# Eight PSUM banks in one ring during the visits of the second feed-forward product

## The chip, the cores and the metric

The kernel runs on one core of one Trainium2 chip. The metric is the device time of one execution in microseconds (us). Three runs of the kernel before gave 1599.46, 1599.53 and 1602.58 us; the median is 1599.53 us. One further execution was profiled, and all views of the trace come from it.

## The reference

The reference is one layer of an encoder, applied to two sequences of 512 tokens with 1024 features each. A normalized input goes through three branches (a state-space scan, a differential attention, a cross attention to a memory), these are gated and merged, and a feed-forward block follows. The change lies in the product with `w_ffn_out`, in the last line of this cut:

```
def _layer(x, mem, l, p):
    ...
    x = x + merged @ p['w_out'][l]
    xn2 = _rmsnorm(x, p['norm_ffn'][l])
    gate, up = jnp.split(xn2 @ p['w_ffn_in'][l], 2, axis=-1)
    return x + (jax.nn.silu(gate) * up) @ p['w_ffn_out'][l]
```

`w_ffn_in` is 1024 x 5632, `w_ffn_out` is 2816 x 1024, all in fp32. The result of the layer is normalized once more and is the output.

## The kernel before

Every fp32 product is made of three matmuls (high x high, high x low, low x high), for which ScalarE casts an operand to its high part (L134, L137) and VectorE subtracts to get the low part (L135, L138). TensorE is called PE below, VectorE DVE, ScalarE ACT, GpSimd POOL, and SP is the engine that issues all DMAs, in one queue.

The two sequences stand side by side as 1024 columns, so that both feed-forward products are 2 x 2 block products. They are done with seven block products in place of eight (a Strassen-Winograd scheme): the list `SEVEN` names them A11, S2, A12, S3, S1, A22, S4. Each of the seven needs a PSUM bank of 128 x 512 fp32 of its own; below they are called products 0 to 6.

- First product (22 steps `i`): seven products of four contraction tiles each. The last step (`i == KFF - 1`) runs its tiles outermost, like a visit, and takes six banks from the ring `mm` and the seventh from the ring `tr` (by `aux()`).
- Second product: twelve *visits* (`VISITS`). A visit is one block of output features with two to four *pairs* of contraction tiles; in each pair all seven products get three matmuls, so a pair is 21 matmuls. Its seven banks are six of `bank()` (ring `mm`) and one of `aux()` (ring `tr`).
- End: the last four contraction tiles, which are no pairs, are done by ordinary tiles of one bank each, over all eight blocks of output features, first for 512 columns, then twice for 256. They take their banks from `bank()`, and each is added to the output `y` by DVE at L1346.

At the end of each visit the seven banks are emptied by `quadrants` (L1104 on): ACT copies product 0 (L1108, `p`), and DVE makes six sums and one second read at L1102, in this order: product 1 (`u`), product 2 (`gf`), product 3 (`u`), product 4 (`p`), product 4 again (`up`), product 5 (`nsq`), product 6 (`nsq`). POOL adds the four results to `y` (L1275).

PSUM has eight banks of this size. Before the change they stand as a ring of six named `mm` and a ring of two named `tr` from the merging stage to the end of the kernel. Because a visit takes six of `mm` and one of `tr`, each `mm` bank comes up again for the product of the same number in the next visit, and a `tr` bank in every second visit. A matmul that opens a bank waits until the last read of what the bank held is done (`reuse_waits="tile"`).

Weights of a pair come from DRAM, in two loads: `wa` (L1225, 384 KB, for A11, A12, A22) and `ws_` (L1223, 512 KB, for the four S). The first 16 pairs are prepared whole, the next 12 in part, the last 8 are split on the spot. A pair's operands `th`, `tl` come from tiles `aD` that the first product wrote to DRAM (L1169) and that are read back at L1121 and L1122.

The order of instructions on each engine is made by a scheduling pass over the program's dependences. For PE, `PE.on = True` holds the order in which the kernel text issues matmuls, from the last step of the first product to the last visit. The other engines' order, and SP's queue, are the pass's own.

Of the kernel before, what the change touches and what calls it, by code (L numbers as in the profile page):

```python
# [72 lines left out]
def encoder(ctx: ExitStack, tc: tile.TileContext, a, out):  # L73
# [19 lines left out]
    def open_banks(**tags):  # L93

        bank_es.close()
        for tag, n in tags.items():
            pools[tag] = bank_es.enter_context(tc.tile_pool(name=tag, bufs=n, space=PSUM, reuse_waits="tile"))

    bank_es = ExitStack()

    open_tags(ctx, ld=4)
    xp_es, phase = ExitStack(), ExitStack()
# [3 lines left out]
    def slot(tag, shape=(P, NT), dt=F32, name="sl"):  # L106
        return pools[tag].tile(list(shape), dt, tag=tag, name=name)

    def bank(tag="mm"):
        return pools[tag].tile([P, 512], F32, tag=tag, name="bk" + tag)  # L110

    def aux():
        return bank("tr")


    ident = cst.tile([P, P], F32, name="ident")
# [14 lines left out]
    def split(hi, lo, src, scale=None):  # L131

        if scale is None:
            h = S.copy(hi, src)  # L134
            l_ = V.tensor_tensor(out=lo, in0=src, in1=hi.bitcast(F32), op=ALU.subtract)  # L135
        else:
            h = S.activation(out=hi, in_=src, func=AF.Copy, scale=scale)  # L137
            l_ = V.scalar_tensor_tensor(out=lo, in0=src, scalar=scale, in1=hi.bitcast(F32), op0=ALU.mult, op1=ALU.subtract)  # L138
        return h, l_
# [47 lines left out]
    def rstd(acc, n, nt=4):  # L187


        ss = aux()  # L190
        for t in range(nt):
            PE.matmul(ss[:, t : t + 1], acc[:, t * P : (t + 1) * P], onec[:, 0:1], start=(t == 0), stop=(t == nt - 1))
        return factor(ss, n, nt)

    def factor(ss, n, nt=4, bias=epsc):

        rs = rp.tile([P, 4], F32, tag="rs", name="rs", bufs=4)
        S.activation(out=rs[:, :nt], in_=ss[:, :nt], func=AF.Sqrt, scale=1.0 / n, bias=bias)
        V.reciprocal(rs[:, :nt], rs[:, :nt])
        bc = aux()  # L200
        for t in range(nt):
            PE.transpose(bc[:, t * P : (t + 1) * P], rs[:, t : t + 1].broadcast_to([P, P]), ident)
        return rs, bc

    open_banks(mm=4, tr=4)
    bD = drp.tile([3, 4, P, NT], F32, name="bD")
    gD = drp.tile([24, P, NT], F32, name="gD")
    mD = drp.tile([4, P, 2, L], F32, name="mD")  # L210
    yD = drp.tile([512, T, NS, NC], F32, name="yD")
    uD = drp.tile([512, T, NS, NC], F32, name="uD")
    kx = Ctx()
    kx.__dict__.update(tc=tc, nc=nc, a=a, slot=slot, open_tags=open_tags, aux=aux, drp=drp, ident=ident, vcol=vcol, uD=uD, yD=yD)
    s5 = s5_gen(kx)
    next(s5)
# [76 lines left out]
    def queued():  # L293

        return tc.issue_after(last_w.ins)
# [286 lines left out]
    memory(1)  # L582

    open_banks(mm=2, sc=3, tr=2, oo=1)
    open_tags(phase, xT=4)
    xa = phase.enter_context(tc.tile_pool(name="xa", bufs=2, reuse_waits="tile"))
# [104 lines left out]
    for i in range(-AHEAD, len(steps) + 1):  # L691
# [14 lines left out]
        if 0 <= i < len(steps):  # L706
# [4 lines left out]
            tr = aux()  # L711
# [215 lines left out]


    open_banks(mm=6, tr=2)
    open_tags(phase, ms=16)  # L930
    ves = ExitStack()
# [46 lines left out]
    def quad_room(i):  # L978
        j = i // 2 % 2
        return slot(f"th{j}", [P, 7, L], F32R, "th"), slot(f"tl{j}", [P, 7, L], F32R, "tl")  # L980
# [3 lines left out]
    def quad_split(i, xa_, xb_, t_):  # L984

        nonlocal last_q
        th, tl = quad_room(i)
        split(th[:, 0], tl[:, 0], xa_[:, 0:L])
        split(th[:, 1:3].rearrange("p a n -> p (a n)"), tl[:, 1:3].rearrange("p a n -> p (a n)"), xb_)
        split(th[:, 3:5], tl[:, 3:5], t_[:, 0:2])  # L990
        last_q = split(th[:, 5:7], tl[:, 5:7], t_[:, 2:4])
        return th, tl
# [112 lines left out]
    def quadrants(ps, p0, other=("up", "gf")):  # L1105

        p1 = ap2.tile([P, L], F32, tag="p1", name="p1")
        S.copy(p1, p0)  # L1108
        u2 = summed("u2", next(ps), p1)
        c11 = summed("gf", next(ps), p1, 2)  # L1110
        u3 = summed("u3", next(ps), u2)
        p5 = next(ps)
        u4 = summed("p1", p5, u2)
        c22 = summed("up", p5, u3, 2)
        c21 = summed(other[0], next(ps), u3, 2)
        return c11, summed(other[1], next(ps), u4, 2), c21, c22

    def act_pair(p, tag="ts", third=PO):

        xa_, xb_ = slot("ld", name="fa"), slot("ld", name="fb")  # L1120
        nc.sync.dma_start(xa_, aD[2 * p])  # L1121
        nc.sync.dma_start(xb_, aD[2 * p + 1])  # L1122
        return xa_, xb_, quad_sums(xa_, xb_, tag, third)
# [60 lines left out]
    def pair_in():  # L1184
        pairs.append(quad_split(len(pairs), *act_pair(len(pairs))))
# [8 lines left out]
    def keep(n):  # L1194
        if not kept:
            lasts.extend(quad_room(NPAIR + 1))
        for _ in range(n):
            i = len(kept)
            if i % 2 == 0:
                lasts[2:] = [slot("ld", [P, 2, L], name="fw")]  # L1200
            k0, k1, raw = lasts
            with queued():
                nc.sync.dma_start(raw[:, i % 2], last_rows(i + 1))
            kept.append((k0[:, i], k1[:, i], raw[:, i % 2]))
# [39 lines left out]
    with queued():  # L1244
        nxt = act_pair(2, third=V)
    n_p = 0
    for v, (m, lo_, hi_) in enumerate(VISITS):
        ps = [bank() for _ in range(6)] + [aux()]
        for p in range(lo_, hi_):
            if n_p + 2 < len(pieces):  # L1250
                next(coming[n_p + 2])
            for g in coming[n_p + 1 : n_p + 2]:
                for _ in g:
                    pass
            th, tl = pairs[p]
            w = made[n_p]
            n_p += 1
            if v < 4 and p == 1:
                with queued():
                    for t in (m, m + 4):  # L1260
                        nc.sync.dma_start(y[t], x1D[t])
            for p_, (nm, o) in zip(ps, SEVEN):
                wh, wl = w[nm]
                PE.matmul(p_, wh, th[:, o], start=(p == lo_), stop=False)
                PE.matmul(p_, wh, tl[:, o], start=False, stop=False)
                PE.matmul(p_, wl, th[:, o], start=False, stop=(p == hi_ - 1))
            if v == 3 and p == 0:
                pair_in()
            if (v, p) in ((10, 7), (10, 8), (11, 7), (11, 8)):
                keep(1 if v == 10 and p == 7 else 2)  # L1270
        ps = iter(ps)
        c11, c12, c21, c22 = quadrants(ps, next(ps), ("nsq", "nsq"))
        for c_, t, s in ((c11, 0, 0), (c22, 4, 1), (c21, 4, 0), (c12, 0, 1)):
            yv = y[m + t][:, s * L : (s + 1) * L]
            PO.tensor_tensor(out=yv, in0=yv, in1=c_, op=ALU.add)  # L1275
        if v == 0:
            with tc.issue_after(last_sum.ins):
                pairs.append(quad_split(2, *nxt))
        elif v == 1:
            with queued(), tc.issue_after(last_sum.ins):  # L1280
                pair_in()
        for _ in range({3: 1, 4: 1, 6: 1, 7: 1}.get(v, 0)):
            pair_in()
        if v == 8:

            r0, r1 = quad_room(NPAIR)
            r2 = slot("ts", [P, 4, L], F32R, name="r2")
            room = [(r0[:, 2 * i : 2 * i + 2], r1[:, 2 * i : 2 * i + 2]) for i in range(3)] + [(r2[:, 0:2], r2[:, 2:4])]
            ah, al = [], []
            for i in range(2 * NPAIR, KFF):  # L1290
                ac = slot("ld", name="fl")
                nc.sync.dma_start(ac, aD[i])
                th, tl = (r_.rearrange("p a n -> p (a n)") for r_ in room[i - 2 * NPAIR])
                split(th, tl, ac, scale=0.5)
                ah.append(th)
                al.append(tl)
    PE.on = False


    def ones(ss, sq, n, start=False, stop=False):  # L1300
# [492 lines left out]
```

## Time and profile before

| | us |
|---|---|
| median of three runs | 1599.53 |
| the profiled execution, its own time | 1599.28 |
| span of its profile | 1597.5 |
| PE busy in it | 1579.1 |
| DVE busy in it | 1163.7 |
| ACT, POOL busy in it | 636.8, 542.6 |
| first matmul of the visits, in us from the span's start | 1360.88 |
| first matmul of the end stage | 1538.82 |

Times in a timeline row are the start in us from the span's start and the length in us; then the engine, the line of the kernel, the operation, what is written from what is read, the shape and the count. In brackets stands how long the engine was idle before, and whose end released it. `bkmm` and `bktr` are banks of the two rings. The length of a matmul is its time through a pipeline: the next starts about 0.23 us after it, so an idle time in brackets is shorter than the step that was lost. `x2` means two neighbours merged into one row.

### The profile page before, as it was taken

Reading aid. Unit: us, or ns where it says so; the run is one execution under the profiler, and the core shown is the slowest. Engines: PE = TensorE matmul, PEld = TensorE weight load, DVE = VectorE, ACT = ScalarE, POOL = GpSimd, SP = SyncE. Lnnn points to the kernel's source line nnn. Section 1 sums busy time; section 2 is a strip of 40 time slices with the busy share of each in tenths; the row PEclk is TensorE's granted clock in tenths of the full one; section 3 lists DMA queues with packets and bytes.
Section 4 is the critical chain, followed back from the end, with each engine's and each line's share of the span. In section 5 each row is a group of like instructions: output and inputs, shape, how many; then the busy total and the mean of one; then the engine's idle time right before and its main releaser. Section 6 shows DMA issues by size and latency. Waiting matters only on the chain.

```text
span 1597.5 us, 21606 instructions
## 1 busy us (share of the span) xinstructions
PE 1579.1 (99%) x7838; PEld 1314.8 (82%) x7838; DVE 1163.7 (73%) x1856; ACT 636.8 (40%) x1140; POOL 542.6 (34%) x449
## 2 busy tenths in 40 slices
PE   9999999999999999999999999999999999999997
PEld 7888788888898789878878878888888888788877
DVE  7976997067774776775365578888898778998654
ACT  6544313265552465573123443323333224233323
POOL 0010100001333220300443366666665553444553
PEclk9999999999999999999999999999999999999999
DMA  9544523676762111253454432333332223985222
GB/s 366 174 159 152 175 94 123 182 261 213 262 224 102 46 55 40 73 178 133 138 190 140 144 108 89 123 122 129 119 116 109 81 91 115 355 332 196 75 67 106
DMA packets 104890, 237.84 MB, mean 149 GB/s; under 512 B 13520, under 2 KB 45008, under 8 KB 104784
## 3 DMA queue, kind: packets, MB, share of 16 engines
q1 hardware_dynamic: 104784, 236.47, 43.4%
q8 instruction: 61, 1.00, 0.2%
q14 instruction: 45, 0.37, 0.1%
HBM read 165.16 MB, written 71.27 MB: 148 GB/s over the span
## 4 chain that ended last, share of the span: by engine, by line
PE 89%; DVE 5%; issue 2%; DMA 2%; POOL 1%; ACT 1%; SPq 0%; POOLq 0%; DVEq 0%; ACTq 0%
PE bkmm L66 78%; PE bktr L66 3%; DVE tl L135 2%; PE bkoo L66 2%; PE bktr L69 2%; PE bksc L66 1%; PE bktr L1627 1%; PE bktr L1598 1%; PE bktr L1688 0%; PE bktr L1686 0%; PE bktr L1687 0%; PE bktr L1566 0%; DMA acc<-in_w_fo 0%; DMA mt<-in_memT 0%; DMA fl<-aD 0%
## 5 line engine op out<-in xcount | busy, mean ns | idle before, releaser
L66 PE MATMUL bkmm<-xh,wh 128*128 128x512 f32 x640 | 254.7, 398 | 0.0
L66 PE MATMUL bkmm<-xh,wl 128*128 128x512 f32 x640 | 251.1, 393 | 0.0
L66 PE MATMUL bkmm<-xl,wh 128*128 128x512 f32 x640 | 250.5, 391 | 0.0
L66 PE MATMUL bkmm<-tl,wh 128*128 128x512 f32 (+1 forms) x621 | 241.3, 389 | 1.4 <-DVE tl L135 1.4
L66 PE MATMUL bkmm<-th,wl 128*128 128x512 f32 (+1 forms) x621 | 241.1, 389 | 1.0 <-DVE wl L135 1.0
L66 PE MATMUL bkmm<-th,wh 128*128 128x512 f32 (+1 forms) x621 | 241.3, 389 | 0.0
L134 ACT CAST wh<-wf 128x1024 fp32r<-128x1024 f32 (+1 forms) x134 | 117.9, 880 | 220.8 <-PE bkmm L66 183.2
L135 DVE TENSOR_TENSOR wl<-wf,wh 128x1024 fp32r<-128x1024 f32 (+1 forms) x134 | 146.5, 1093 | 48.8 <-ACT wh L134 33.5
L66 PE MATMUL bkmm<-th,w 128*128 128x512 f32 x432 | 141.4, 392 | 3.5 <-DVE up L1102 2.0
L66 PEld LDWEIGHTS bkmm<-xh,wl 128*128 128x128 f32 x640 | 120.2, 188 | 26.6 <-issue 1.3
L66 PEld LDWEIGHTS bkmm<-xh,wh 128*128 128x128 f32 x640 | 120.4, 188 | 26.4 <-issue 3.4
L66 PEld LDWEIGHTS bkmm<-xl,wh 128*128 128x128 f32 x640 | 120.5, 188 | 22.6 <-issue 0.4
L66 PEld LDWEIGHTS bkmm<-tl,wh 128*128 128x128 f32 x621 | 116.6, 188 | 26.2 <-DVE tl L135 2.1
L66 PEld LDWEIGHTS bkmm<-th,wl 128*128 128x128 f32 x621 | 116.6, 188 | 25.6 <-DVE wl L135 1.9
L66 PEld LDWEIGHTS bkmm<-th,wh 128*128 128x128 f32 x621 | 116.6, 188 | 23.7
L1166 POOL TENSOR_TENSOR up<-up,acc 128x512 f32<-128x512 f32 x44 | 84.2, 1931 | 87.4 <-DVE up L1102 87.4
L454 POOL TENSOR_TENSOR raw<-raw 128x128 f32<-128x128 f32 x28 | 15.2, 546 | 285.0 <-DVE nb L545 206.5
L66 PEld LDWEIGHTS bkmm<-th,w 128*128 128x128 f32 x432 | 80.9, 188 | 24.9 <-DVE up L1102 4.5
L793 POOL TENSOR_TENSOR mg<-mg,gl 128x1024 f32<-128x1024 f32 x16 | 43.5, 2720 | 138.1 <-DVE gl L789 138.1
L66 PE MATMUL bkmm<-tl,w 128*128 128x512 f32 x216 | 84.2, 390 | 0.0
L66 PE MATMUL bkmm<-yh,wh 128*128 128x512 f32 x192 | 75.9, 397 | 0.8 <-DVE gl L789 0.8
L1165 ACT ACTIVATE ac<-gf 128x512 f32<-128x512 f32 x44 | 27.8, 633 | 122.5 <-DVE gf L1164 63.5
(651 smaller groups left out, 3580.8 us busy)
## 6 DMA issues: line engine op xcount, KB each, us to landing
wf<-in_w_in SPq DMA_DIRECT2D x40, 512.0 KB, 4.1
wD<-hl SPq DMA_DIRECT2D x28, 512.0 KB, 2.9
w<-wD SPq DMA_DIRECT2D x28, 512.0 KB, 4.8
gD<-gt SPq DMA_DIRECT2D x24, 512.0 KB, 2.8
gl<-gD SPq DMA_DIRECT2D x24, 512.0 KB, 3.4
wf<-in_w_fg SPq DMA_DIRECT2D x22, 512.0 KB, 3.7
wf<-in_w_fu SPq DMA_DIRECT2D x22, 512.0 KB, 3.6
aD<-ac SPq DMA_DIRECT2D x22, 512.0 KB, 3.0
```

Of the source, the lines that this page charges most:

```text
L66: return self.put(self.eng.matmul(*args, **kw))
L69: return self.put(self.eng.transpose(*args, **kw))
L134: h = S.copy(hi, src)
L135: l_ = V.tensor_tensor(out=lo, in0=src, in1=hi.bitcast(F32), op=ALU.subtract)
L454: PO.tensor_tensor(out=a22, in0=a21, in1=a22, op=ALU.add)
L793: PO.tensor_tensor(out=mg[m], in0=mg[m], in1=gt, op=ALU.add)
L1165: last_t = S.activation(out=ac[:, cs], in_=gf, func=AF.Tanh, scale=0.5)
L1166: PO.tensor_tensor(out=up, in0=up, in1=accs[s], op=ALU.mult)
L1598: PE.matmul(kp[64 * hf : 64 * hf + 48, g * 144 : (g + 1) * 144], l_[:, 2 * hf + g, :], o_[:, 4 * g4 + 2 * hf + g, :], start=(l_ is lr48), ...
L1627: PE.matmul(ps[:, g * P : (g + 1) * P], w_[:, gg * P : (gg + 1) * P], u_[:, 8 * o + gg, :], start=True, stop=True)
```

## The change

All eight banks are opened as one ring `mm` before the first visit, `aux()` takes from it while there is no `tr`, and after the last visit the rings of six and two are opened again.

```diff
     def open_banks(**tags):
 
         bank_es.close()
+        open_now.clear()
+        open_now.update(tags)
         for tag, n in tags.items():
...
-    bank_es = ExitStack()
+    bank_es, open_now = ExitStack(), {}
...
     def aux():
-        return bank("tr")
+        return bank("tr" if "tr" in open_now else "mm")
...
     n_p = 0
+    open_banks(mm=8)
     for v, (m, lo_, hi_) in enumerate(VISITS):
...
     PE.on = False
+    open_banks(mm=6, tr=2)
```

No arithmetic changes. A ring that is opened anew starts at its own first bank; it does not go on where the ring before it stood. In the built program PE's matmuls stand in the same order as before. At two places of the visits DVE, ACT, POOL and SP have a few instructions in another order: around the step from the first visit to the second, and around the step from the fourth to the fifth.

## The prediction

> **What bounds the kernel now.** I read the page's busy times first, then the waits of PE within the visits, then PE's and DVE's timelines at each place where a bank is used again.
>
> ```profile
> span 1597.5 us, 21606 instructions
> ...
> PE 1579.1 (99%) x7838; PEld 1314.8 (82%) x7838; DVE 1163.7 (73%) x1856; ACT 636.8 (40%) x1140; POOL 542.6 (34%) x449
> ```
>
> PE is busy all but 18.4 us of the span. A change that moves no matmul can win only from those 18.4 us, and it loses wherever it makes a new wait on PE. Which of them lie in the visits (1358 to 1546 us) the view of waits tells; its columns are total, number of waits, and longest:
>
> ```profile
> PE bkmm L66 <- DVE up L1102: 2.0, 3, 1.0
> PE bkmm L66 <- DVE wl L135: 1.0, 1, 1.0
> PE bkmm L66 <- ACT w L137: 0.7, 1, 0.7
> PE bkmm L66 <- DVE u L1102: 0.4, 1, 0.4
> PE bkmm L66 <- DVE w L138: 0.4, 1, 0.4
> ```
>
> Only the first row is a wait for a bank: `up` is the second read of product 4. Rows with `w` and `wl` wait for weights. The change can remove the first row and what of the same kind is too short for this view.
>
> PE's timeline shows the size. Two pairs of one visit with no wait:
>
> ```profile
> 1386.75 0.39 PE L66 MATMUL bkmm<-th,w 128*128 128x512 f32 x1
> ...
> 1391.51 0.39 PE L66 MATMUL bkmm<-th,w 128*128 128x512 f32 x1
> ```
>
> That is 4.76 us for 21 matmuls, a step of 0.227 us, or 0.68 us per product. The first pairs of six visits do worse, each time at the first matmul of product 4:
>
> ```profile
> 1373.64 0.40 PE L66 MATMUL bkmm<-th,w 128*128 128x512 f32 x1
> 1375.04 0.50 PE L66 MATMUL bkmm<-th,w 128*128 128x512 f32 x1 [1.00 <-DVE up L1102]
> 1375.38 0.40 PE L66 MATMUL bkmm<-tl,w 128*128 128x512 f32 x1
> ...
> 1403.52 0.74 PE L66 MATMUL bkmm<-th,w 128*128 128x512 f32 x2
> 1404.10 0.39 PE L66 MATMUL bkmm<-tl,w 128*128 128x512 f32 x1
> ...
> 1422.70 0.39 PE L66 MATMUL bkmm<-th,w 128*128 128x512 f32 x1
> 1423.54 0.50 PE L66 MATMUL bkmm<-th,w 128*128 128x512 f32 x1 [0.46 <-DVE up L1102]
> ...
> 1466.35 0.94 PE L66 MATMUL bkmm<-th,w 128*128 128x512 f32 x2
> 1467.13 0.40 PE L66 MATMUL bkmm<-tl,w 128*128 128x512 f32 x1
> ...
> 1481.01 0.39 PE L66 MATMUL bkmm<-th,w 128*128 128x512 f32 x1
> 1481.98 0.50 PE L66 MATMUL bkmm<-th,w 128*128 128x512 f32 x1 [0.58 <-DVE up L1102]
> ...
> 1530.79 0.95 PE L66 MATMUL bkmm<-th,w 128*128 128x512 f32 x2
> 1531.57 0.40 PE L66 MATMUL bkmm<-tl,w 128*128 128x512 f32 x1
> ```
>
> A step longer than 0.23 us is lost time, and the step after a wait takes 0.34, so a restart costs 0.11 more. Second visit: 1.40 - 0.23 + 0.11 = 1.28 us. Fifth: 0.84 - 0.23 + 0.11 = 0.72. Ninth: 0.97 - 0.23 + 0.11 = 0.85. Eighth and twelfth: two steps take 0.78 in place of 0.46, so 0.32 each. Fourth: one step of 0.34 (1403.76 to 1404.10), 0.11. In all 3.60 us.
>
> **The change, part by part.**
>
> *Between visits.* With seven banks of a ring of eight, product n of a visit takes the bank that product n-1 of the visit before held; product 0 takes one long free. So product 4 no longer waits for the second read of product 4 but for the read of product 3, and the late read now stands before product 5, 0.68 us later in PE's order. The second visit shows what that is worth:
>
> ```profile
> 1372.33 0.67 DVE L1102 TENSOR_TENSOR u<-bkmm,u 128x512 f32<-128x512 f32 x1
> ...
> 1374.31 0.68 DVE L1102 TENSOR_TENSOR up<-bkmm,u 128x512 f32<-128x512 f32 x1
> ```
>
> The read of product 3 ended at 1373.00, before PE wanted product 4 (1373.87). Product 5 would then be wanted at 1374.55, and its bank is free at 1374.99: without more, 0.44 of the wait would stay. But the opening (below) makes PE arrive here 2.39 us later, while the DVE work in front of these reads does not wait for PE, so I count the whole 1.28 us as gone. The fourth (0.11) and the fifth (0.72) go too: in the fifth, product 5 is wanted at 1422.70 + 4 x 0.227 = 1423.61, and the row names `up` as ended by 1423.5. At the ninth something stays:
>
> ```profile
> 1481.25 0.68 DVE L1102 TENSOR_TENSOR up<-bkmm,u 128x512 f32<-128x512 f32 x1
> ```
>
> It ends at 1481.93. This DVE work hangs on a chain begun before the eighth visit's wait, so it does not gain that visit's 0.32. PE wants product 5 at 1481.01 + 0.91 - 0.32 = 1481.60 and gets it at 1481.98: 0.38 + 0.11 stay of 0.32 + 0.85, so 0.68 is won in both. The 0.32 of the twelfth is lost again at once, since PE next waits for `w` (last row of the waits). Won: 1.28 + 0.11 + 0.72 + 0.68 = 2.79 us. Ends: nothing beyond the second visit, 1.28, if DVE and the loads do not follow PE; 3.60 if all follows.
>
> *The opening.* The new ring starts at its own first bank, not behind the last one used. In the built program the first visit's products 0, 1 and 2 get the banks that held product 0 of the first product's last step, nothing, and product 6 of that step. Product 6 is read last of all, as the ring's wait tells:
>
> ```profile
> 1364.42 0.68 DVE L1102 TENSOR_TENSOR gf<-bktr,p 128x512 f32<-128x512 f32 x1
> ```
>
> ```profile
> 1362.64 0.63 PE L66 MATMUL bkmm<-th,w 128*128 128x512 f32 x2
> ```
>
> The second matmul of PE's row, at 1362.87, opens product 2. It may now start only when DVE is done at 1365.10, plus 0.05 (1374.99 to 1375.04 above): 1365.15. DVE is late because of work queued in front of this read, and that has no reason to move. New wait 2.28 + 0.11 = 2.39 us. Products 3 to 6 use banks read earlier than 1365.10. Ends: 2.39, or nothing if the order on DVE frees the bank in time, for which I see no cause.
>
> *The closing.* The reopened ring starts at the bank that held product 3 of the last visit; before, it was that of product 0. Here DVE is far behind, with splits queued in front of the reads:
>
> ```profile
> 1538.82 0.39 PE L66 MATMUL bkmm<-th,wh 128*128 128x512 f32 x1
> 1539.05 0.39 PE L66 MATMUL bkmm<-tl,wh 128*128 128x512 f32 x1
> 1540.39 0.50 PE L66 MATMUL bkmm<-th,wl 128*128 128x512 f32 x1 [0.96 <-DVE wl L135]
> ...
> 1542.83 0.39 PE L66 MATMUL bkmm<-th 128*128 128x512 f32 x1
> ```
>
> ```profile
> 1542.07 0.67 DVE L1102 TENSOR_TENSOR u<-bkmm,u 128x512 f32<-128x512 f32 x1
> ```
>
> Before, the first end tile begins at 1538.82, waits for `wl` inside, and the second begins at 1542.83. Now the first may begin only after the read of product 3, at 1542.74 + 0.05 = 1542.79; its twelve matmuls with a restart take 12 x 0.227 + 0.11 = 2.83, and the second begins at 1545.62. Its bank held product 6, which DVE reads two sums and a second read later, 4 x 0.60 us after product 3: 1545.14, in time. New wait: 1545.62 - 1542.83 = 2.79 us; the wait for `wl` is inside it. Nothing after it on PE waits long enough to give it back: the chain of the end stage is PE itself. Ends: 2.79, and some 0.3 less if DVE follows the twelfth visit's gain.
>
> *The queues.* In SP's order the store of the last `aD` tile (L1169) moves ahead of the weights of the second visit's second pair, together with four small loads; the `y` loads move behind them.
>
> ```profile
> 1374.41 0.32 SPq L1169 DMA_DIRECT2D aD<-ac  x1
> ```
>
> ```profile
> w<-wD SPq DMA_DIRECT2D x3, 512.0 KB, 6.7
> w<-wD SPq DMA_DIRECT2D x4, 384.0 KB, 5.2
> ```
>
> The store waits for DVE's last two `ac` instructions, which the new order puts ahead of the first visit's reads: some three steps of 0.60 after 1369.93, about 1371.8. The weights behind it are issued from about 1372.2, and with a landing of 5.2 us for the first (1377.4) and 6.7 for the second (1379.3) they meet a PE that wants them at 1371.11 + 2.39 + 4.76 = 1378.3 and 0.7 us later. The store in front leaves the DMA engines emptier than in these rows, so I take 0; the ends are 0 and +1.0. ACT's copy of product 0 moves behind two casts and ends near 1372.2, where product 1, whose bank that is, comes at 1374.2: covered by the opening's wait. POOL's adds to `y` start some 7 us later, and the next visit's reads need its `nsq` buffers only around 1388.
>
> *Sum.* 1599.28 (profiled execution) + 2.39 - 2.79 + 2.79 = 1601.7 us. That execution lies 0.25 below the median shown.
>
> **The rivals.**
>
> *The clock falls (slower).* The closing leaves PE without a matmul from 1538.82 to 1542.79, 3.97 us, where the longest gap of the visits now is 1.4. At the end of the kernel the granted clock (PEclk, the column after the busy times) fell:
>
> ```profile
> 1590.20 0.40 PE L69 MATMUL bktr<-ident,rs 128*128 128x128 f32 x2 [0.64 <-DVE rs L199]
> ```
>
> ```profile
> 1589.00:1592.50 3.50, 0.96 (x6) 0.66 (x6) 1.79 (x6) 0.63 (x2) 2.22 (x5) 0.91 0.80 280
> 1592.50:1597.00 4.50, 0.00 (x0) 0.00 (x0) 0.59 (x2) 0.00 (x0) 0.68 (x1) 0.50 0.66 233
> ```
>
> 0.91 over 3.5 us is 0.63 us at half clock, so it fell at about 1591.9, 2.9 us after sparse work began at 1589. If PE stays slow for as long after the closing, half of it is lost, 1.5 us: 1603.2. The Trainium skill, "TensorE: Matmul & The Clock Gate" (Part 1), puts the fall to half clock after an idle window of about 3.4 us that runs free, and the return after a busy one; an estimate by it is 1.7 us lost in place of 1.5, in those runs where the window falls into the gap. Chance 0.30.
>
> *The edges cost nothing (faster).* If the banks of the two edges were free in time, only the 2.79 won would remain: 1596.5. For it: nothing but the gain. Against it: both reads stand in DVE's row after work that does not depend on PE. It decides if the two edges together cost under the 2.79 won. The Trainium skill, "Perfetto Trace Analysis", section "Matmul Optimizations", asks that all eight PSUM banks be put to use; by that alone this would be the outcome, 1596.5 in place of 1601.7. No row of before shows a ring of eight. Chance 0.05.
>
> *The gains do not come (slower).* If DVE and DMA set the visits' pace, only the second visit's 1.28 is won: 1599.28 + 2.39 + 2.79 - 1.28 = 1603.2. For it: DVE is the releaser of every wait named. Against it: its splits wait in turn for operand room that PE frees. Chance 0.08.
>
> *The second visit's weights are late.* 1602.7 with the +1.0 above, on the bound itself. Chance 0.07, half to each side.
>
> **How the numbers follow.** The forecast of 1601.7 (own range 1600.6, with 3.60 won and 0.3 less at the closing, to 1602.7, with the +1.0) has 0.50. A measurement can tell about 0.2%, 3.2 us, from no change: 1596.3 to 1602.7. Faster 0.05 from the second rival, whose 1596.5 lies at the edge of what counts as faster; slower 0.30 + 0.08 + 0.035, rounded to 0.40; within 0.55. The range of 8 in 10 leaves out the faster rival. Its low end takes the 1600.6 and two DVE steps of 0.60 that come earlier at one edge, 1599.4; its high end takes the clock rival and the +1.0, 1604.2.
>
> **What would show it.** Right: PE waits about 2.3 us in the first visit for `gf` of the last step, none for `up` in the second and fifth visits, a rest under 0.5 in the ninth, and a wait of about 4 us at the first end tile for `u`. Wrong: no wait at either edge, a wait for `w` or a DMA in the second visit's second pair, or a PEclk below 1 around the first end tiles.

## The result, and the profile after

The changed kernel takes 1607.41 us (median of 6 runs, 1607.03 to 1609.98), the kernel before beside it 1599.93 (6 runs). The ratio is 1.0044, with an interval of 1.0034 to 1.0054: slower by some 7 us. The forecast was 1601.7 with a range of 1599.4 to 1604.2, so the measured time lies outside. The profiled execution took 1607.21 us; the sums of this section are made against that and the 1599.28 of the profiled execution before.

The head of the page after:

```profile
span 1605.4 us, 21608 instructions
...
PE 1582.4 (99%) x7838; PEld 1316.8 (82%) x7838; DVE 1164.9 (73%) x1856; ACT 637.0 (40%) x1140; POOL 540.7 (34%) x449
```

PE is busy for 3.3 us more with the same 7838 matmuls. Waits alone do not do that: some matmuls have become slower. The waits of PE from the visits to the first end tiles (total, number, longest):

```profile
PE bkmm L66 <- DVE u L1104: 3.9, 1, 3.9
PE bkmm L66 <- DVE gf L1104: 2.1, 1, 2.1
PE bkmm L66 <- DVE up L1104: 1.7, 2, 1.1
PE bkmm L66 <- ACT w L139: 0.6, 1, 0.6
PE bkmm L66 <- DVE w L140: 0.4, 1, 0.4
PE bkmm L66 <- DMA w<-wD: 0.2, 1, 0.2
```

`u` and `gf` are the two edges, both where the prediction put them. But the row with `up`, which the change was to remove, has only gone from 2.0 to 1.7.

PE at the opening, and at the closing up to the second end tile (the last row, `bkmm<-th`, is its first matmul):

```profile
1362.61 0.40 PE L66 MATMUL bkmm<-th,w 128*128 128x512 f32 x1
1365.13 0.50 PE L66 MATMUL bkmm<-th,w 128*128 128x512 f32 x1 [2.13 <-DVE gf L1104]
...
1540.86 0.39 PE L66 MATMUL bkmm<-th,w 128*128 128x512 f32 x1
1545.13 0.76 PE L66 MATMUL bkmm<-th,wh 128*128 128x512 f32 x1 [3.88 <-DVE u L1104]
1545.69 0.63 PE L66 MATMUL bkmm<-tl,wh 128*128 128x512 f32 x1
1546.12 0.63 PE L66 MATMUL bkmm<-th,wl 128*128 128x512 f32 x1
...
1550.39 0.63 PE L66 MATMUL bkmm<-th 128*128 128x512 f32 x1
```

After the gap the steps are 0.43 us in place of 0.23. The view by windows shows the granted clock (PEclk, the third figure from the right):

```profile
1540.50:1544.00 3.50, 0.75 (x4) 0.28 (x2) 3.50 (x7) 0.28 (x1) 0.00 (x0) 1.00 0.00 0
1544.00:1547.50 3.50, 2.37 (x6) 1.92 (x7) 3.38 (x6) 0.00 (x0) 2.51 (x2) 0.54 0.00 0
1547.50:1551.00 3.50, 3.50 (x10) 2.73 (x9) 0.38 (x1) 0.00 (x0) 2.51 (x3) 0.50 0.00 0
1551.00:1554.50 3.50, 3.50 (x17) 2.87 (x16) 1.00 (x2) 0.66 (x2) 0.00 (x0) 0.98 0.00 0
```

A mean of 0.54 over 3.5 us is half clock from 1544.28 on, 0.98 in the last stretch is half clock until 1551.1: 6.8 us at half clock.

The sum of the difference, read at PE's first matmul of each part: the visits begin 0.17 us later; the first visit takes 2.15 us longer; the other eleven visits together 0.05 less; from the end of the visits to the third end tile (1541.09 to 1553.49, before 1538.82 to 1545.55) it is 12.40 in place of 6.73, 5.67 more. That makes 7.94, and the spans differ by 7.9. After the third end tile nothing changes.

What each visit loses beyond its pairs at 4.76 us, from the first matmul of the visit to that of the next, is the table on which most of the experiments are read (us; the kernels are told below):

| visit | 1 | 2 | 4 | 5 | 6 | 8 | 9 | 10 | 11 | 12 | all |
|---|---|---|---|---|---|---|---|---|---|---|---|
| before | 0.71 | 1.36 | 0.14 | 0.78 | 0.03 | 0.38 | 0.85 | 0 | 1.29 | 1.04 | 6.58 |
| changed | 2.86 | 0.46 | 0.02 | 1.39 | 0.37 | 0 | 0.90 | 0 | 1.62 | 1.06 | 8.68 |
| both edges mended | 0.94 | 0.85 | 0.01 | 1.31 | 0.30 | 0 | 0.75 | 0 | 1.00 | 1.08 | 6.24 |
| the same, reads first | 0.98 | 0.90 | 0 | 0 | 0 | 0 | 0 | 1.75 | 0.95 | 1.09 | 5.67 |
| the same, and a third room | 1.66 | 0.36 | 0 | 0 | 0 | 0 | 0 | 1.73 | 0 | 0 | 3.75 |
| before, a third room alone | 2.28 | 0.12 | 0.05 | 0.79 | 0.02 | 0.35 | 0.72 | 0 | 0 | 0 | 4.33 |

(The third and seventh visit lose nothing in any of them.)

### The profile page after: what moved, and what is told of

It is laid out like the page before. It is cut to its first block, busy times and chain, and to the rows that moved or that the text cites. A ratio compares the mean times of both kernels' runs of the same rounds, so it can differ in the third digit from the quotient of the medians.

```text
span 1605.4 us, 21608 instructions
## 1 busy us (share of the span) xinstructions
PE 1582.4 (99%) x7838; PEld 1316.8 (82%) x7838; DVE 1164.9 (73%) x1856; ACT 637.0 (40%) x1140; POOL 540.7 (34%) x449
## 4 chain that ended last, share of the span: by engine, by line
PE 85%; DVE 4%; issue 4%; DMA 3%; POOL 2%; ACT 1%; SPq 0%; POOLq 0%; DVEq 0%; ACTq 0%
PE bkmm L66 75%; PE bktr L66 2%; PE bkoo L66 2%; PE bktr L69 2%; DVE tl L137 2%; PE bksc L66 1%; PE bktr L1631 1%; POOL mg L795 1%; DMA yt<-bD 1%; PE bktr L1602 1%; DMA w<-wD 1%; DMA acc<-in_w_fo 1%; PE bktr L1691 0%; PE bktr L1692 0%; PE bktr L1690 0%
## 5 line engine op out<-in xcount | busy, mean ns | idle before, releaser
L66 PE MATMUL bkmm<-th,w 128*128 128x512 f32 x504 | 158.0, 392 | 5.3 <-DVE gf L1104 2.1
L66 PEld LDWEIGHTS bkmm<-th,w 128*128 128x128 f32 x504 | 94.4, 188 | 29.6 <-DVE up L1104 3.0
L66 PE MATMUL bkmm<-tl,w 128*128 128x512 f32 x252 | 98.1, 389 | 0.0
```

What stands on the lines that cost most here:

```text
L66: return self.put(self.eng.matmul(*args, **kw))
```

## The experiments

Each was timed beside the kernel before on the same chip. That kernel's median there was 1598.0 to 1600.5 us, so ratios and differences count, not times across groups.

### The two edges, apart and together

Three kernels take the eight banks one by one in an order that is written out, so that it alone decides which bank a product gets. Instructions stand on PE, DVE, ACT and POOL as in the changed kernel; SP has one load ahead of one store, and two loads exchanged.

```diff
-    open_banks(mm=8)
+    open_banks(**{f"q{i}": 1 for i in range(8)})
+    RING = (0, 7, 4, 5, 3, 2, 1, 6)
     for v, (m, lo_, hi_) in enumerate(VISITS):
-        ps = [bank() for _ in range(6)] + [aux()]
+        ps = [pools[f"q{RING[(7 * v + j) % 8]}"].tile([P, 512], F32, tag="q", name="bkmm") for j in range(7)]
```

This one (`t_open`) mends the opening alone.

> The eight banks in an order in which products 0 to 6 of the first visit find banks that are read early, while the first two end tiles still get the banks of products 3 and 6 of the last visit, as in the changed kernel. If the two edges and the clock are the whole cost: the wait for `gf` in the first visit goes (2.2 us), the wait of 3.9 us before the end stage and the slow clock after it stay: 1607.1 - 2.2 = 1604.9. Rival, that PE's delay at the opening is what spoilt the visits: their 2.7 us of gains come back as well, 1602.2.

Measured: ratio 1.0035 (1.0022 to 1.0048), 5.4 us above the kernel before (1603.79 to 1598.38). That answers to the first expectation (1604.9 is 5.6 above 1599.28), not to the rival (2.9). Its two longest waits:

```profile
PE bkmm L66 <- DVE u L1104: 3.9, 1, 3.9
PE bkmm L66 <- DMA w<-wD: 2.1, 1, 2.1
```

The wait for `gf` is gone, that for `u` stays. In the profiled execution a wait for weights stands in place of `gf`, in the first visit's second pair; it lost 2.66 us in this visit all the same. The load landed at 1368.92, 8.63 us after its issue. It does not land so late each time: in `t_open_fill` below, whose loads stand in the same order, it took 6.64 us; the first visit lost 0.67 there, but the second lost 1.91 to later loads and other short waits. So part of what the bank's wait costs is cover for waits that PE meets right behind it, and how much differs from one execution to the next.

With `RING = (5, 7, 6, 4, 0, 3, 2, 1)` (`t_close`) the opening stays as in the changed kernel and the first end tile finds the free bank.

> The order of the eight banks as in the changed kernel for the opening (product 2 of the first visit takes the late bank), but the first end tile finds the free bank and the second that of product 3. If the gap before the end stage causes both the wait and the slow clock: 1607.1 - 2.8 (wait) - 2.8 (clock) = 1601.5, PEclk 1.0 around the first end tiles. Rival, that the slow matmuls of the first end tile have another cause than the gap: only the wait goes, 1604.3.

Measured: 1.0011 (1.0002 to 1.0020), 2.1 us above the kernel before (2.2 expected). The wait for `u` and the slow matmuls both go; the first end tile begins at 1539.08, and PEclk is 1.00 around it:

```profile
1539.00:1542.00 3.00, 2.06 (x10) 1.37 (x9) 3.00 (x6) 0.00 (x0) 0.00 (x0) 1.00 0.00 0
1542.00:1546.00 4.00, 4.00 (x19) 3.05 (x18) 3.96 (x7) 0.00 (x1) 3.04 (x3) 1.00 0.00 0
```

The edge and nothing in the end stage itself was their cause.

With `RING = (5, 7, 4, 3, 0, 2, 1, 6)` (`t_both`) both edges are mended.

> Both edges given early banks, the ring of eight otherwise the same. If edges and clock are the whole cost and the visits gain nothing net: 1599.3, as before the change. Rival, that the visits gain what the prediction said once PE enters them on time: 1596.6. Rival, that the ring of eight itself makes the visits worse: over 1600.5.

Measured: 1.0007 (0.9998 to 1.0016), 0.8 us above. The first expectation holds; the 1596.6 that the prediction's gains would give does not come, and the visits are not worse either (6.24 in the table, before 6.58). Between the three, by medians, the closing costs 4.6 us (1603.79 less 1599.15) and the opening 1.3 (1600.45 less 1599.15). Counted from the changed kernel's 7.5 us above instead, they are 5.4 (7.5 less 2.1) and 2.1 (7.5 less 5.4).

### Wait or clock

The closing has two parts. 17 matmuls in its gap, into the bank that is free and with a result that is not used, keep PE busy but leave the wait for the bank as it is:

```diff
+    fi = bank()
+    for _ in range(17):
+        PE.matmul(fi, wh, th[:, o], start=True, stop=True)
     PE.on = False
     open_banks(mm=6, tr=2)
```

In the changed kernel (`e_fill`):

> The changed kernel with 17 more matmuls (3.9 us of PE) into the bank that is free, put between the last visit and the end stage; their result is not used. The first end tile still waits for product 3 until about the same moment. If the gap lowers the clock, the first end tiles run at full clock: 1607.1 - 2.8 = 1604.3. If the slow matmuls have another cause: 1607.1, unchanged.

Measured: 1.0037 (1.0023 to 1.0050), 5.9 us above, where 5.0 would have answered to 1604.3 and 7.8 to 1607.1; the interval (3.7 to 8.0 us) holds both, so the trace must decide. The clock after the visits stays at 1.0: the gap lowers it. But in the profiled execution it fell at the other edge, after the wait of 2.1 us for `gf`:

```profile
1362.59 0.40 PE L66 MATMUL bkmm<-th,w 128*128 128x512 f32 x1
1365.08 0.51 PE L66 MATMUL bkmm<-th,w 128*128 128x512 f32 x1 [2.09 <-DVE gf L1104]
```

```profile
1362.50:1365.00 2.50, 0.49 (x3) 0.05 (x1) 2.50 (x5) 0.00 (x0) 1.03 (x1) 1.00 0.99 379
1365.00:1369.50 4.50, 4.42 (x12) 3.50 (x13) 4.19 (x7) 2.83 (x5) 1.49 (x2) 0.62 0.65 242
1369.50:1373.00 3.50, 3.50 (x17) 2.86 (x16) 3.20 (x6) 2.56 (x4) 0.00 (x0) 1.00 0.26 81
```

0.62 over 4.5 us is 3.4 us at half clock, 1.7 us lost. In the changed kernel's profile the same gap (2.13) left the clock at 1.0. So the opening's price differs from one execution to the next.

The same filling in `t_open`, where there is no wait for `gf` (`t_open_fill`):

> The run whose opening was mended and whose closing was left, with 17 more matmuls in the gap before the end stage, into the free bank; their result is not used. The wait for the bank stays as it is, only PE is not idle in it. If the gap lowers the clock and that costs 2.8 us: PEclk 1.0 after the last visit, and 2.6 us above the kernel before in place of 5.4. If the closing's price is all in the wait: 5.4 above it.

Measured: 1.0026 (1.0016 to 1.0036), 4.3 us above, where `t_open` was 5.4 above; the intervals overlap, so the times alone do not settle the size. The trace does:

```profile
1537.50:1541.00 3.50, 3.50 (x17) 2.88 (x17) 3.50 (x7) 0.00 (x0) 0.00 (x0) 1.00 0.00 0
1541.00:1544.50 3.50, 3.47 (x16) 2.56 (x15) 3.06 (x6) 0.00 (x0) 2.84 (x3) 1.00 0.00 0
```

From the end of the visits (1537.76) to the third end tile (1547.37) it takes 9.61 us: 2.88 more than before the change, and 2.79 less than the 12.40 of the changed kernel. So the wait costs 2.88 us (2.79 predicted), the clock another 2.79. With the 0.8 that `t_both` stands above, the 2.88 make 3.7 of the 4.3 measured; the rest is within the interval.

### Why the visits gain nothing

In the table the fifth visit has become worse (0.78 to 1.39), the ninth no better. DVE and POOL at the end of the fourth visit, after the change:

```profile
1420.97 1.40 DVE L974 TENSOR_TENSOR ts<-fa 128x512 f32<-128x512 f32 x1
...
1423.50 1.40 DVE L976 TENSOR_TENSOR ts<-fb,ts 128x512 f32<-128x512 f32 x1
...
1425.42 0.68 DVE L1104 TENSOR_TENSOR up<-bkmm,u 128x512 f32<-128x512 f32 x1
```

```profile
1420.53 1.30 POOL L975 TENSOR_TENSOR ts<-fb,fa 128x512 f32<-128x512 f32 x1 [5.37 <-DVE tl L137]
1423.06 1.29 POOL L1278 TENSOR_TENSOR y<-y,gf 128x512 f32<-128x512 f32 x1 [1.23 <-DVE gf L1104]
```

And DVE before the change:

```profile
1420.41 0.68 DVE L974 TENSOR_TENSOR ts<-fb,ts 128x512 f32<-128x512 f32 x1
...
1422.20 0.68 DVE L975 TENSOR_TENSOR ts<-fb,ts 128x512 f32<-128x512 f32 x1
1422.80 0.69 DVE L1102 TENSOR_TENSOR up<-bkmm,u 128x512 f32<-128x512 f32 x1
```

And POOL beside that first sum, before the change:

```profile
1420.57 1.67 POOL L1275 TENSOR_TENSOR y<-y,gf 128x512 f32<-128x512 f32 x1
```

The pass has put the sums of the next pair's operands (`ts`) in other places among the reads. There they meet POOL, which starts first: two sums of 0.68 us take 1.40, each ending some 0.55 us after the POOL operation beside it (1421.83 to 1422.37, 1424.35 to 1424.90). The read `up` ends 4.59 us after the visit's start in place of 3.28. From the visit's first read to `up` there are as many DVE operations as before, so the delay is that of the two longer sums (0.72 each), not more work. Before, the sum at 1420.41 started ahead of POOL, and it was POOL's add that took 1.67, where the same add takes 1.29 after the change. The Trainium skill, "SBUF — State Buffer" (SBUF: two separate sides), says that DVE with two SBUF inputs and GpSimd take a shared pair of ports in turn, each for a whole instruction. These rows agree; no run here takes POOL away alone.

The ninth visit has another cause, for there the order on DVE is that of before. DVE's reads stand behind a split (`r`) that waits for a load:

```profile
1481.00 1.06 ACT L139 ACTIVATE r<-fl 128x1024 fp32r<-128x1024 f32 x1 [3.86 <-DMA fl<-aD]
1482.09 1.23 DVE L140 SCALAR_TENSOR_TENSOR r<-fl,r 128x1024 fp32r<-128x1024 f32 x1 [2.37 <-ACT r L139]
```

The load landed at 1480.92, 0.53 us after the visit's first matmul; before the change it landed 0.19 us ahead of it (1478.33).

To take the order out of the question, `pair_in()` is put behind the reads on DVE in the changed order of banks (`t_both_reads`), and in the kernel before (`b_reads`):

```diff
         for _ in range({3: 1, 4: 1, 6: 1, 7: 1}.get(v, 0)):
-            pair_in()
+            with tc.issue_after(last_sum.ins):
+                pair_in()
```

> As the run with both edges mended, and the sums and splits of the next pair's operands are put behind the reads of the banks on DVE after the fourth, fifth, seventh and eighth visit. If the visits gained nothing because DVE reaches the reads late: the 1.29 + 0.30 + 0.75 us that the fifth, sixth and ninth visits still lose go, 2.3 us in all; with both edges mended the kernel stood 0.8 us above the one before, so now 1.5 below it. Rival, that the operands become late instead: a wait of PE for `th` or `tl`, and no gain.

Measured: 1.0001 (0.9992 to 1.0009). The 2.3 us of the fifth, sixth and ninth visits go, as the table shows, but the kernel does not come out below the one before. PE from the tenth visit on:

```profile
PE bkmm L66 <- ACT w L139: 1.0, 2, 0.6
PE bkmm L66 <- DVE wl L137: 0.9, 1, 0.9
PE bkmm L66 <- DVE w L140: 0.4, 1, 0.4
PE bkmm L66 <- DVE up L1104: 0.2, 1, 0.2
```

The tenth visit, which lost nothing, now loses 1.75: it begins at 1496.66, with both edges mended at 1498.78, and PE reaches its weights earlier than they are ready. Three of these four rows are weights. In the tenth visit ACT, which casts them, had waited for POOL's sums, and these stand behind POOL's adds to `y`:

```profile
1507.37 0.63 ACT L139 ACTIVATE w<-acc 128x512 fp32r<-128x512 f32 x1 [4.08 <-POOL acc L459]
```

The rival that the gain is given back came true, with `w` in the place of `th`.

> The kernel before (rings of six and two) with only this order on DVE: reads of the banks ahead of the next pair's sums and splits. If the order on DVE is the whole cause of the waits in the fifth, eighth and ninth visits: 0.72 + 0.32 + 0.85 = 1.9 us below the kernel before, without the ring of eight. If the ring is what is lacking: within 0.5 us of the kernel before.

Measured: 1.0006 (0.9997 to 1.0015), 0.7 us above. The gain of 1.9 us is not there, and 0.7 lies just outside the other expectation's 0.5, though the interval (-0.5 to 2.4 us) holds it. Here too the fifth, eighth and ninth visits lose nothing, and the tenth to twelfth lose 4.2 us in place of 2.3.

### A third room for raw weights

The last weights are loaded raw, summed by POOL, and cast and subtracted by ACT and DVE, in two rooms (`acc`). A third room for every third load:

```diff
     open_tags(phase, yo=4)
+    rawp, n_raw = phase.enter_context(tc.tile_pool(name="raw", bufs=1, reuse_waits="tile")), []
...
-            raw = new_acc().rearrange("p (a n) -> p a n", n=P)
+            n_raw.append(p)
+            raw = (new_acc() if len(n_raw) % 3 else rawp.tile([P, L], F32, tag="raw", name="acc")).rearrange("p (a n) -> p a n", n=P)
```

> As the run with both edges mended and the reads first on DVE, and a third room for the raw weights that are summed and split during the visits (every third load takes it). In that run the tenth visit lost 0.45 + 1.29 us, waiting among others for `w`, and POOL had waited 9.6 us for a room to be free. If the rooms set the pace of the last visits and so took the gain back: these 1.7 us go, some 1.6 us below the kernel before. Rival, that ACT's and DVE's order sets it: no better than the run with two rooms, +0.1 from the kernel before.

Measured: 0.9984 (0.9975 to 0.9993), 2.8 us below the kernel before. The gain is there, but not in the place named: the tenth visit still loses 1.73, and POOL still waits 9.6 us once. No run moves POOL's work in front of that visit's weights. What goes is the 0.95 and 1.09 of the eleventh and twelfth visits and the wait for `wl` in the first end tile.

> The kernel before (rings of six and two) with the reads first on DVE and the third room, without the ring of eight. If the ring of eight is what lets the visits run without waits for banks: the second visit (1.28 us) and the waits in the ninth and tenth stay, and it is at least 1 us above the run with ring, reads and room. If the ring adds nothing: the same as that run within 0.5 us.

Measured: 0.9983 (0.9975 to 0.9992), 2.4 us below. The ring of eight adds nothing that can be measured.

> The kernel before with the third room for raw weights alone: rings of six and two, DVE's order as it was. If the room is what pays by itself (it took the waits for `w` and `wl` from the eleventh visit on): 2 to 2.5 us below the kernel before, as much as with the reads first. If the two are needed together: less than 1 us below it, since the waits for `up` in the visits stay.

Measured: 0.9983 (0.9974 to 0.9993), 3.1 us below, without ring and without the new order on DVE. PE from the ninth visit to the end of the kernel:

```profile
PE bktr L66 <- ACT nsq L1362: 0.7, 1, 0.7
PE bktr L69 <- DVE rs L199: 0.6, 1, 0.6
PE bkmm L66 <- DVE up L1102: 0.4, 1, 0.4
```

The rows `wl` (1.0), `w` (0.7) and `w` (0.4) of the kernel before are gone, and with them the 1.29 and 1.04 us of its last two visits and the 0.96 inside the first end tile: 3.3 us, about what the time shows. With the third room the pass also sets raw loads earlier in SP's queue and a few instructions of DVE, ACT and POOL in another order; no run parts the two. The first visit loses 1.57 more than before, and the second 1.24 less: the weights of the first visit's second pair landed 8.24 us after their issue (before, 6.69). `t_open` and `t_open_fill` show both lengths with loads in one order, so this is not laid to the room. This version beats both kernels of the case, and the two with the new order besides do no better.

### One ring from the first product to the end

`e_whole` opens the ring of eight before the first product and keeps it; `e_whole_reads` has the reads first as well.

```diff
-    open_banks(mm=6, tr=2)
+    open_banks(mm=8)
     open_tags(phase, ms=16)
...
-    open_banks(mm=8)
     for v, (m, lo_, hi_) in enumerate(VISITS):
...
     PE.on = False
-    open_banks(mm=6, tr=2)
```

> One ring of eight opened before the first feed-forward product and kept to the end of the kernel, so that there is no edge at all. If edges and clock are the cost: none of the waits for `gf` and `u`, PEclk 1.0, and the 0.96 us wait for `wl` in the first end tile is filled by the second end tile, whose bank is free: about 1 us below the kernel before. Rival, that the ring of eight costs elsewhere (the first product, the order of the end stage): above it.

> The ring of eight without edges, and DVE's reads ahead of the next pair's operands. If both causes are right they add: about 1.0 + 2.0 = 3 us below the kernel before. Rival: one of the two gains is given back by late weights or operands, then it is no better than the run without the new order on DVE.

Measured: 1.0107 (1.0094 to 1.0121) and 1.0107 (1.0091 to 1.0122), 17.4 and 16.6 us above. There is indeed no edge at the visits, but the rival came true: the ring that carries the small tiles too costs more elsewhere. Waits of PE in `e_whole`, in the first product and in the end stage:

```profile
PE bkmm L69 <- DVE rs L201: 5.6, 2, 4.9
```

```profile
PE bkmm L66 <- DVE acc L184: 3.9, 2, 2.4
PE bkmm L66 <- POOL acc L184: 1.4, 1, 1.4
```

Before the change `rs` has one wait of 0.6 us in `bktr` in the end stage, and the others are not there. By these rows PE now waits for the operands of the small products of the norms, which took their banks from the ring `tr` before; why the pass puts them where PE must wait was not tried. The longest of these waits lowered the clock too, as at the closing:

```profile
960.00:965.00 5.00, 1.23 (x5) 1.23 (x6) 4.54 (x7) 1.14 (x3) 5.00 (x8) 0.75 0.31 108
965.00:970.00 5.00, 5.00 (x14) 3.90 (x14) 1.97 (x2) 0.91 (x2) 5.00 (x5) 0.57 0.01 2
```

That is 2.5 and 4.3 us at half clock, 6.8 together. The visits begin 8.6 us late (1369.46) and lose 4.96 us in all, 1.3 less than with both edges mended; the rest of the time goes in the end stage, where the clock fell again (0.81 from 1575 to 1580).

## Why the prediction was wrong

**The opening: right.** The wait for `gf` came at product 2, 2.13 us by the trace, and the first visit takes 2.15 us longer (2.39 said). What it did not see is that PE meets other waits right behind this one: the first two visits lose 3.32 us in the changed kernel, and with the opening mended still 1.79 (`t_both`), 2.58 (`t_open_fill`) and 2.66 (`t_open`), where before the change they lose 2.07. By the medians taking the wait away wins 1.3 to 2.1 us.

**The closing: the wait right, its clock not counted.** The term was 2.79; the wait measures 2.88. But the gap also halved the clock, for 2.79 more, and for that the sum had nothing: this is one of the two steps that failed. The clock fell in both profiled kernels that kept this gap idle (the changed kernel and `t_open`). The prediction had it as a rival at 1.5 us and 0.30. It took the time at half clock to be as long as the fall takes, 2.9 us; it was 6.8. That rival had the mechanism right and its size at half.

**Between the visits: wrong.** This is the other step that failed: "Won: 2.79 us". The measured gain is 0.05. The 2.74 missing here and the 2.79 of the clock are the 5.5 us between the sum's 1601.7 and the 1607.21 of the profiled execution, about half each. Of the term's parts, the second visit wins 0.90 (1.28 said; no wait for `up` is left there, but one for weights), the fourth 0.12 (0.11); the fifth loses 0.61 where 0.72 was to be won, the eighth and ninth win 0.33 in place of 0.68, and the sixth and eleventh, not in the sum, lose 0.34 and 0.33. The mechanism of the ring holds: product 5 is now the one that waits for the late read. Wrong was to take that read's time from the trace of before. The order on DVE around the step from the fourth to the fifth visit had changed; the description of the change says so, and the prediction did not price it. In the ninth visit the order had not changed, but a load in front of the reads came later. And beyond it lies the larger error: even with these waits gone (`t_both_reads`), PE runs into weights that are not ready. Those of the last two visits and of the first end tile came late for want of a third room; those of the tenth stand behind POOL's sums, which no run moved. The rows `w` and `wl`, set aside as waits that the change cannot remove, were what would take its gain.

**The rivals.** "The gains do not come" was close in kind, at 0.08, with 1.28 left to the second visit; the runs show why. It came together with the falling clock, and the prediction had no case for both: 1599.28 + 2.39 + 2.79 - 1.28 + 1.5 would have been 1604.7. "The second visit's weights are late" came at 0.46, one pair later than said: a load for the third pair landed at 1383.91, inside that pair. "The edges cost nothing" did not come: both edges cost about what the sum said.

## What to carry to other kernels

A wait on PE is worth its length only if the next thing PE needs is ready as much earlier; before costing its removal, look up what PE would wait for next (here weights behind two rooms), and mend that first: it was worth 3.1 us by itself. Where a pool of banks is opened anew in the middle of a stream, compare for each bank the last read by the old order with the first use by the new one, and count on an idle gap of PE costing more than its length: the gap of 3.9 us did so in both kernels that kept it, one of 2.1 us in one execution of three. And rates and read times taken from a trace hold only where the order on the reading engine has stayed.

## What the runs showed of the hardware that was not expected

The half clock came in steps of one length. It lasted 3.4 us after the opening's gap in `e_fill`, and 6.8 us after the closing's gap in the changed kernel and in `t_open` (1542.4 to 1549.2) and after the 4.9 us wait in `e_whole`. In the changed kernel PE was still idle for the first 0.85 us after the fall (1544.28 to 1545.13), and the clock came back not at the first multiple of 3.4 us but at the second. The Trainium skill, "TensorE: Matmul & The Clock Gate" (Part 1), has a window of 3413 ns that runs free, a fall after an idle one and a return after a busy one. The lengths agree. The Trainium skill, "TensorE: Matmul & The Clock Gate" (Why this matters for your kernels), advises against idle gaps above some 3 us. Here a gap of 2.1 us halved the clock in one execution of three that were profiled with it (`e_fill`, but not the changed kernel or `t_close`), and one of 2.1 us for weights in `t_open` did not. So a window of 3.4 us need not be wholly idle. How much of it must be idle, these gaps do not settle.
